# Second feed-forward layer on one core: order of the sums of factors, of the copies of finished blocks, and of the last scaling

## The chip, the cores and the metric

The kernel runs on one core of a Trainium2 chip. The core has five engines with queues of their own: TensorE (PE: matmuls, and PEld for loading their weights), VectorE (DVE), ScalarE (ACT), GpSimd (POOL) and SyncE (SP), which here issues most transfers. Sixteen DMA engines move data between the main memory and the core's SBUF; matmuls write to PSUM, which has eight banks of 128 x 512 float32 numbers. The metric is the device time of one execution in microseconds (us), given as the median of several runs.

## The reference

The program is one layer of a diffusion trunk: a mixer with a gated linear recurrence, then a feed-forward part with a convolution, each with a normalisation ahead and a gated residual behind, and a last normalisation. Only the end matters here:

```python
def conv_ffn(h, w_up, conv_w, conv_b, w_down):
    u = dwconv(h @ w_up, conv_w, conv_b)
    gate, val = jnp.split(u, 2, axis=-1)
    return (jax.nn.silu(gate) * val) @ w_down

def rmsnorm(x, g):
    xf = x.astype(jnp.float32)
    y = xf * lax.rsqrt(jnp.mean(xf * xf, axis=-1, keepdims=True) + EPS)
    return (y * g).astype(x.dtype)
...
    lat = lat + g2 * conv_ffn(hl, ffn_w_up[l], ffn_conv_w[l], ffn_conv_b[l], ffn_w_down[l])
...
return rmsnorm(lat, final_g)
```

The second feed-forward layer is the product with `w_down`: 2048 tokens x 2816 by 2816 x 1024. The result is multiplied by the gate g2, added to the residual stream, normalised over its 1024 columns and scaled by `final_g`.

## The kernel before

**A product in seven.** The matrix of hidden values (2048 x 2816) and `w_down` (2816 x 1024) are each cut in two by two blocks. Instead of eight block products the kernel makes seven, from sums and differences of blocks (a scheme of the Strassen kind). Tokens are dealt to the two row blocks by tiles of 128: even tiles to one, odd tiles to the other. A block product is 1024 x 1408 by 1408 x 512.

**Steps and phases.** The inner dimension of 1408 is cut into `NC` = 11 slices of 128. One slice of one block product is a *step*. The first six products are phases 0 to 5, so steps 0 to 65 (`for s in range(N)`, L1721, `ph, c = divmod(s, NC)`). In a step a *left factor* (128 x 1024: the transposed hidden values of eight token tiles) meets a *right factor* (128 x 512). There are eight output blocks `ys[j]` of 128 x 512, one in each PSUM bank. The seventh product runs last, in another order: block after block, each in a piece of eight slices and one of three (`pieces`, L1755), so that each block of tokens can be finished and stored while the next is computed.

**High and low parts.** A float32 factor is split in a high part (rounded, by ACT, L78) and a low part (what the rounding left, by DVE, L79). `product` (L1634) makes three matmuls of it: high by high (L1637), high by low (L1638), low by high (L1639). The tiles are called `mh` and `ml` for the left factor, three buffers each, and `wd` for the right one, both parts in one tile. While the first two matmuls of a step run, the low part of its left factor may still be missing; the third one needs it.

**Sums.** In phases 1 to 3 the left factor is the sum or difference of two blocks (L1598, tiles `S` and `lr`; `lr` has four buffers, and phase 3 needs two a step). In phases 1, 2, 3 and 5 the right factor is a difference (L1627, tiles `rr` and `u2`, two buffers each); in phases 1 and 2 the difference is also stored by SP (L1629), for a later phase. All these sums are made by DVE, in place.

**Run-ahead.** `ahead(s)` (L1710) is traced once a step, before the products of the step. It traces the loads of left factors up to step s+3 and of right ones up to step s+5, then the left factors up to s+2 (`make_left`, L1595) and the right ones up to s+4 (`make_right`, L1624). The order in which each engine issues is not the order of the text: a planner goes through the program with its own estimates of durations and issues, on each engine, what is ready first, with the earlier text first among what is ready. So a sum, whose inputs come from memory, can be queued well ahead of a low part that stands earlier in the text, and once queued it holds its engine until its inputs are there: the engines issue in the planned order.

**End of a phase.** `phase_end` (L1666) empties the eight blocks: in phases 0 to 3 ACT copies them (to `P`, `X`, `V` and tiles `lr`), in phases 4 and 5 DVE adds them to `P` and `X`. Phases 1, 2 and 3 go on in the banks of the phase before, adding to what is there, so that they can write block j only when block j has been copied; phases 0, 4 and 5 start afresh, in banks that must have been emptied. What is to be done afterwards with each block (a subtraction, gate and residual, squares) is put into the list `later` and traced one item a step.

**The end.** `finish` (L1656) sums the two squares, makes the scale with one multiplication and addition on DVE and one power on POOL (`rms_scale`, L72), then scales both halves of a token tile on DVE (L1663, times scale, times `final_g`) and stores each by SP (L1664). Even tiles are finished after their last piece (L1774 to L1778), odd ones through `later`.

Of the kernel before, what the change touches and what calls it, by code (L numbers as in the profile page):

```python
# [11 lines left out]
F32 = mybir.dt.float32  # L12
# [3 lines left out]
AF = mybir.ActivationFunctionType  # L16
OP = mybir.AluOpType
# [4 lines left out]
D = 1024  # L22
# [7 lines left out]
EPS = 1e-6  # L30
# [15 lines left out]
def body(ctx, tc, a, out):  # L46
    nc = tc.nc
    pe, act, dve, pool, sp = nc.tensor, nc.scalar, nc.vector, nc.gpsimd, nc.sync
# [20 lines left out]
    mhalf = small("mhalf")  # L69
# [7 lines left out]
    def split(h, l, src):  # L77
        i = act.activation(h, src, AF.Copy)  # L78
        j = dve.tensor_tensor(l, src, h.bitcast(F32), OP.subtract)  # L79
        return i.ins, j.ins  # L80
# [955 lines left out]
    NC = NFF // 2  # L1036
# [312 lines left out]
    wk = pool_(fa, "wka", 2)  # L1349
# [152 lines left out]
    for g, (half, s, n, q, pairs) in enumerate(todo):  # L1502
# [3 lines left out]
        w, r = pairs[q].w.pop(LEFT[n]), rhs[n]  # L1506
        if n == "B11":
            z = bank["a", q] = ps.tile([128, HJ, 128], F32, name="za", tag="za")
# [3 lines left out]
        elif n == "T2":  # L1512
            z = ps.tile([128, HJ, 128], F32, name="zb", tag="zb")
            acc_mm(z, w, r, True)
            dve.tensor_tensor(u2s[q], u2s[q], z, OP.add)
        elif n == "T1":
            z = bank["d", q] = ps.tile([128, HJ, 128], F32, name="zd", tag="zd")
# [3 lines left out]
        elif n == "T3":  # L1521
            z = bank["c", q] = ps.tile([128, HJ, 128], F32, name="zc", tag="zc")
            acc_mm(z, w, r, True)
            dve.tensor_tensor(cols(uvs[q], 1), cols(uvs[q], 1), z, OP.add)  # L1524
        elif n == "B21":
            z = bank["a", q]
# [26 lines left out]
    def gate_rows():  # L1553
# [32 lines left out]
    def left_split(s, width, src, **kw):  # L1586
        h = mk.tile([128, HALF], F32R, name="mh", tag="mh", bufs=3)
        l = mk.tile([128, HALF], F32R, name="ml", tag="ml", bufs=3)
        lefts[s] = h, l
        h, l = h[:, 0:width], l[:, 0:width]  # L1590
        if kw:
            h, l = [v.rearrange("p (c n) -> p c n", **kw) for v in (h, l)]
        split(h, l, src)

    def make_left(s, raw):  # L1595
        ph = s // NC
        if 1 <= ph <= 3:
            dve.tensor_tensor(raw[0], raw[0], raw[1], OP.add if ph == 1 else OP.subtract)  # L1598
# [25 lines left out]
    def make_right(s, raw):  # L1624
        ph, c = divmod(s, NC)
        if len(raw) > 1:
            dve.tensor_tensor(raw[0], raw[0], raw[1], OP.subtract)  # L1627
            if ph < 3:
                sp.dma_start(t_d[ph - 1][c], raw[0])  # L1629
        if ph > 4:  # L1630
            gate2(ph - 5, raw[0])
        right_split(s, raw[0])

    def product(z, l, r, start, stop):  # L1634

        (lh, ll), (rh, rl) = l, r
        pe.matmul(z, lh, rh, start=start, stop=False, skip_group_check=True)  # L1637
        pe.matmul(z, lh, rl, start=False, stop=False, skip_group_check=True)  # L1638
        pe.matmul(z, ll, rh, start=False, stop=stop, skip_group_check=True)  # L1639
# [4 lines left out]
    def residual2(t, dh, v):  # L1644

        cs = slice(dh * 512, (dh + 1) * 512)
        lat = wk.tile([128, 512], F32, name="latd", tag="latd", bufs=3)
        sp.dma_start(lat, lat_d[t][:, cs])
        gate2(dh, v)
        dve.tensor_tensor(v, v, lat, OP.add)  # L1650

    def square(t, dh, v):
        sq = wk.tile([128, 512], F32, name="sq", tag="sq", bufs=1)
        act.activation(sq, v, AF.Square, accum_out=sums[:, dh, t:t + 1])

    def finish(t, vs):  # L1656
        ss = wk.tile([128, 1], F32, name="ssf", tag="ssf", bufs=2)
        rs = wk.tile([128, 1], F32, name="rsf", tag="rsf", bufs=2)
        dve.tensor_tensor(ss, sums[:, 0, t:t + 1], sums[:, 1, t:t + 1], OP.add)
        rms_scale(rs, ss, 1, D)  # L1660
        for i, v in enumerate(vs):
            cs = slice(i * 512, (i + 1) * 512)
            dve.scalar_tensor_tensor(v, v, rs, st["fg"][:, cs], OP.mult, OP.mult)  # L1663
            sp.dma_start(out[t * 128:(t + 1) * 128, cs], v)  # L1664

    def phase_end(ph, ys):  # L1666

        for j, z in enumerate(ys):
            if ph == 0:
                act.activation(P[:, j], z, AF.Copy)  # L1670
            elif ph == 1:
                act.activation(X[:, j], z, AF.Copy)  # L1672
                later.append(lambda j=j: dve.tensor_tensor(X[:, j], P[:, j], X[:, j], OP.subtract))
            elif ph == 2:
                act.activation(V[:, j], z, AF.Copy)
                later.append(lambda j=j: residual2(2 * j, 1, V[:, j]))
            elif ph == 3:
                if j % 2 == 0:
                    st["w", j] = st["w", j + 1] = left_raw()
                w = st["w", j][:, j % 2 * 512:(j % 2 + 1) * 512]  # L1680
                act.activation(w, z, AF.Copy)
                st["c22", j] = w

                def c22(j=j, w=w):
                    dve.tensor_tensor(X[:, j], X[:, j], w, OP.add)
                    residual2(2 * j + 1, 0, X[:, j])
                    residual2(2 * j + 1, 1, w)
                    square(2 * j + 1, 1, w)
                later.append(c22)
            elif ph == 4:  # L1690
                dve.tensor_tensor(P[:, j], P[:, j], z, OP.add)  # L1691

                def c11(j=j):
                    residual2(2 * j, 0, P[:, j])
                    square(2 * j, 0, P[:, j])
                later.append(c11)
            else:
                dve.tensor_tensor(X[:, j], X[:, j], z, OP.add)

                def c21(j=j):  # L1700
                    square(2 * j + 1, 0, X[:, j])
                    finish(2 * j + 1, (X[:, j], st["c22", j]))
                later.append(c21)

    later = []
    raws_l = {s: None for s in range(2)}
# [3 lines left out]
    def ahead(s):  # L1710
        for t in range(len(raws_l), min(s + 4, N if s >= 4 else 6)):
            raws_l[t] = load_left(t)
        for t in range(len(raws_r), min(s + 6, N + NC)):
            raws_r[t] = load_right(t)
        for t in range(len(lefts), min(s + 3, N)):
            make_left(t, raws_l[t])
        for t in range(len(rights), min(s + 5, N + NC)):
            make_right(t, raws_r[t])

    S = V = None  # L1720
    for s in range(N):  # L1721
        ph, c = divmod(s, NC)
        if s == 4:
            for f in pending:
                f()
            fa.close()
            wk = pool_(fb, "wkb")
            S = wk.tile([128, NC, HT, 128], F32, name="S")
        if s == 4 * NC // 2:
            V = h2p.tile(ST, F32, name="V", tag="rB21", bufs=1)  # L1730
        if s == NC // 2 + 1:
            st["g2"], st["fg"], gate_bias = gate_rows()
        if s == 2 * NC - 2:
# [30 lines left out]
    for i, (j, cs) in enumerate(pieces):  # L1764
        prepare_last(i + 2)
        if cs.start == 0:
            z = ps.tile([128, 512], F32, name="y", tag="y")
        l = lefts[N + i]
        for n, c in enumerate(cs):
            js = slice(n * 128, (n + 1) * 128)  # L1770
            product(z, [v[:, js] for v in l], rights[N + c], c == 0, c == NC - 1)
        if later and i % 2 == 0:
            later.pop(0)()
        if cs.start:  # L1774
            v = V[:, j]
            dve.tensor_tensor(v, v, z, OP.add)  # L1776
# [30 lines left out]
```

## Time and profile before

| | us |
|---|---|
| median of 3 runs | 2758.75 |
| the runs | 2753.68 to 2759.02 |
| the profiled execution | 2759.34 |
| its span in the profile | 2757.3 |
| first matmul of this stage starts | 2322.7 |
| last matmul starts | 2749.84 |
| TensorE busy, whole span | 2708.4 (98%) |
| DVE busy, whole span | 1976.0 (72%) |
| ACT busy, whole span | 1129.5 (41%) |

The stage thus takes 427 us of the 2757. Rows of the profile name the engine, the line of the kernel, the operation and what it writes and reads (`ml<-S,mh` writes ml from S and mh). In the view in order of time the first number is the start, the second the duration, and a bracket at the end says how long the engine stood idle before and what released it. In the view of groups, `xN | busy, mean ns | idle before` follow the shape. In the view of waits, the numbers are us in total, how often, and the longest. The view of windows gives the busy time of each engine in a stretch. The granted clock of TensorE is full throughout. Matmuls overlap: each is shown at 0.39 us, but a new one starts every 0.227 us.

### The profile page before, as it was taken

Reading aid. Unit: us, or ns where it says so; the run is one execution under the profiler, and the core shown is the slowest. Engines: PE = TensorE matmul, PEld = TensorE weight load, DVE = VectorE, ACT = ScalarE, POOL = GpSimd, SP = SyncE. Lnnn points to the kernel's source line nnn. Section 1 sums busy time; section 2 is a strip of 40 time slices with the busy share of each in tenths; the row PEclk is TensorE's granted clock in tenths of the full one; section 3 lists DMA queues with packets and bytes.
Section 4 is the critical chain, followed back from the end, with each engine's and each line's share of the span. In section 5 each row is a group of like instructions: output and inputs, shape, how many; then the busy total and the mean of one; then the engine's idle time right before and its main releaser. Section 6 shows DMA issues by size and latency. Waiting matters only on the chain. (4 is left out here: it accounts for less than half of the span.)

```text
span 2757.3 us, 42014 instructions
## 1 busy us (share of the span) xinstructions
PE 2708.4 (98%) x16060; PEld 2254.6 (82%) x16060; DVE 1976.0 (72%) x2791; ACT 1129.5 (41%) x1885; POOL 568.2 (21%) x885
## 2 busy tenths in 40 slices
PE   6999999999999999999999999999999999999998
PEld 4888888888888888888887888888888888877887
DVE  4756655566666776668886887777877777586886
ACT  4424443333233233335665444444444444333343
POOL 2111111011111111211220533443434440000001
PEclk9999999999999999999999999999999999999999
DMA  5213323224534443228888222228322234987563
GB/s 230 92 51 100 104 85 100 85 71 168 172 123 136 149 137 112 86 84 295 298 305 323 92 92 68 86 77 305 93 72 81 77 92 151 319 294 249 186 194 122
DMA packets 229104, 410.56 MB, mean 149 GB/s; under 512 B 29604, under 2 KB 137508, under 8 KB 225064
## 3 DMA queue, kind: packets, MB, share of 16 engines
q1 hardware_dynamic: 224584, 398.13, 43.6%
q10 hardware_dynamic: 4320, 9.77, 0.9%
q8 instruction: 126, 2.06, 0.3%
q14 instruction: 74, 0.61, 0.1%
HBM read 293.23 MB, written 114.57 MB: 148 GB/s over the span
## 5 line engine op out<-in xcount | busy, mean ns | idle before, releaser
L445 PE MATMUL z<-tok,w 128*128 128x512 f32 x1280 | 515.4, 403 | 0.0
L447 PE MATMUL z<-tok,w 128*128 128x512 f32 x1280 | 501.0, 391 | 0.0
L446 PE MATMUL z<-tok,w 128*128 128x512 f32 x1280 | 500.8, 391 | 0.0
L79 DVE TENSOR_TENSOR w<-raw,w 128x512 fp32r<-128x512 f32 (+1 forms) x260 | 239.6, 925 | 138.0 <-ACT w L78 134.0
L447 PEld LDWEIGHTS z<-tok,w 128*128 128x128 f32 x1280 | 240.4, 188 | 51.8
L445 PEld LDWEIGHTS z<-tok,w 128*128 128x128 f32 x1280 | 240.7, 188 | 46.0 <-issue 1.7
L446 PEld LDWEIGHTS z<-tok,w 128*128 128x128 f32 x1280 | 241.1, 188 | 45.0 <-DVE tok L79 0.9
L78 ACT ACTIVATE w<-raw 128x512 fp32r<-128x512 f32 (+1 forms) x260 | 196.0, 759 | 138.9 <-PE zd L1061 77.4
L1639 PE MATMUL y<-wd,ml 128*128 128x512 f32 x600 | 234.4, 391 | 2.8 <-DVE ml L79 2.7
L1637 PE MATMUL y<-wd,mh 128*128 128x512 f32 x600 | 233.8, 390 | 2.6 <-ACT X L1672 1.8
L1638 PE MATMUL y<-wd,mh 128*128 128x512 f32 x600 | 233.5, 389 | 0.0
L514 DVE TENSOR_TENSOR_SCAN S<-F,d 128x528 f32<-128x528 f32 (+1 forms) x80 | 91.5, 1143 | 113.3 <-ACT F L496 113.2
L79 DVE TENSOR_TENSOR w<-s,w 128x512 fp32r<-128x512 f32 x126 | 121.3, 968 | 52.8 <-ACT w L78 52.0
L1058 PE MATMUL zc<-rT,w 128*128 128x512 f32 x352 | 137.1, 389 | 1.2 <-DVE uv L1524 1.0
L1060 PE MATMUL zc<-rT,w 128*128 128x512 f32 x352 | 136.9, 389 | 0.0
L1061 PE MATMUL zc<-rT,w 128*128 128x512 f32 x352 | 136.9, 389 | 0.0
L1639 PEld LDWEIGHTS y<-wd,ml 128*128 128x128 f32 x600 | 112.6, 188 | 29.3 <-DVE ml L79 5.9
L1637 PEld LDWEIGHTS y<-wd,mh 128*128 128x128 f32 x600 | 112.6, 188 | 27.0 <-ACT X L1672 2.2
L78 ACT ACTIVATE w<-s 128x512 fp32r<-128x512 f32 x126 | 78.2, 627 | 137.6 <-POOL s L1114 81.0
L75 POOL TENSOR_TENSOR rs<-rs,mhalf 128x1 f32<-128x1 f32 (+3 forms) x53 | 61.7, 1165 | 345.0 <-DVE rs L74 345.0
L1638 PEld LDWEIGHTS y<-wd,mh 128*128 128x128 f32 x600 | 112.6, 188 | 23.2
L1058 PE MATMUL za<-rB,w 128*128 128x512 f32 x336 | 130.7, 389 | 0.0
(353 smaller groups left out, 6246.8 us busy)
## 6 DMA issues: line engine op xcount, KB each, us to landing
raw<-in_w_up_dram SPq DMA_DIRECT2D x88, 512.0 KB, 4.1
raw<-in_w_in_dram SPq DMA_DIRECT2D x80, 512.0 KB, 4.0
lr<-m SPq DMA_DIRECT2D x49, 512.0 KB, 6.0
m<-r SPq DMA_DIRECT2D x66, 256.0 KB, 4.1
spare<-in_w_ada_dram SPq DMA_DIRECT2D x32, 512.0 KB, 4.3
kq<-stash SPq DMA_DIRECT2D x15, 1024.0 KB, 7.8
og<-stash SPq DMA_DIRECT2D x30, 512.0 KB, 5.3
u<-in_w_down_dram SPq DMA_DIRECT2D x51, 256.0 KB, 4.2
```

Source lines behind the costliest of these rows:

```text
L78: i = act.activation(h, src, AF.Copy)
L79: j = dve.tensor_tensor(l, src, h.bitcast(F32), OP.subtract)
L445: pe.matmul(z, w[:, 0, k], h, start=k == 0, stop=False, skip_group_check=True)
L446: pe.matmul(z, w[:, 0, k], l, start=False, stop=False, skip_group_check=True)
L447: pe.matmul(z, w[:, 1, k], h, start=False, stop=k == KT - 1, skip_group_check=True)
L514: dve.tensor_tensor_scan(flat(S[:, d]), flat(F[:, d]), flat(d1[:, 0:ns]), 0.0, OP.mult, OP.max)
L1058: pe.matmul(o, w[:, 0, k], r[:, :, 0, k], start=start and k == 0, stop=False, skip_group_check=True)
L1060: pe.matmul(o, w[:, 0, k], r[:, :, 1, k], start=False, stop=False, skip_group_check=True)
L1061: pe.matmul(o, w[:, 1, k], r[:, :, 0, k], start=False, stop=k == 3, skip_group_check=True)
L1637: pe.matmul(z, lh, rh, start=start, stop=False, skip_group_check=True)
L1638: pe.matmul(z, lh, rl, start=False, stop=False, skip_group_check=True)
L1639: pe.matmul(z, ll, rh, start=False, stop=stop, skip_group_check=True)
```

## The change

Three things are changed, all in the second feed-forward layer.

1. *Sums tied behind the last low part.* `left_split` now keeps the instruction that makes the low part. A left or right sum, and in phases 0 to 3 the item of `later` too, is traced inside `behind_left()`: its DVE instructions may not be issued ahead of the low part that was traced last. `tc.issue_after(i)` adds an order within i's engine, no wait for its end. With the order of the text, the left sum of step s+3 comes behind the low part of step s+2, and the right sum of step s+4 behind the low part of step s+2.
2. *Finished blocks one by one.* `phase_end` takes one block and is traced directly behind that block's last product, in place of all eight behind the step. Its instruction for block 7 is kept, and all that the next `ahead` traces on the same engine (ACT after phases 0 to 3, DVE after phase 4) is tied behind it. No item of `later` is traced in the last step of a phase.
3. *Last scaling.* `last_finish` takes the place of addition, square and `finish` for the even tiles. P's half is multiplied by `final_g` ahead of the scale; the first square's part of the scale is made ahead; V's half is multiplied by `final_g` into a tile of its own after the addition; the scale is then one DVE operation and the power; DVE scales V's half and SP stores it, ACT scales P's half and stores it from its own queue.

```diff
+    made_left, ended = [], []
+
+    def behind_left():
+        return tc.issue_after(made_left[-1]) if made_left else ExitStack()
...
-        split(h, l, src)
+        made_left.append(split(h, l, src)[1])
 
     def make_left(s, raw):
         ph = s // NC
         if 1 <= ph <= 3:
-            dve.tensor_tensor(raw[0], raw[0], raw[1], OP.add if ph == 1 else OP.subtract)
+            with behind_left():
+                dve.tensor_tensor(raw[0], raw[0], raw[1], OP.add if ph == 1 else OP.subtract)
...
         if len(raw) > 1:
-            dve.tensor_tensor(raw[0], raw[0], raw[1], OP.subtract)
+            with behind_left():
+                dve.tensor_tensor(raw[0], raw[0], raw[1], OP.subtract)
...
-    def phase_end(ph, ys):
-
-        for j, z in enumerate(ys):
-            if ph == 0:
-                act.activation(P[:, j], z, AF.Copy)
...
+    def phase_end(ph, j, z):
+
+        if ph == 0:
+            i = act.activation(P[:, j], z, AF.Copy)
...
+        return i.ins
...
         if s >= 2:
-            ahead(s)
+            with ExitStack() as tied:
+                for i in ended:
+                    tied.enter_context(tc.issue_after(i))
+                ended.clear()
+                ahead(s)
...
             product(ys[j], [v[:, js] for v in l], r, c == 0 and ph in (0, 4, 5), c == NC - 1)
+            if c == NC - 1:
+                ended[:] = [phase_end(ph, j, ys[j])]
...
-        if later:
-            later.pop(0)()
-        if c == NC - 1:
-            phase_end(ph, ys)
+        if later and c < NC - 1:
+            with behind_left() if ph < 4 else ExitStack():
+                later.pop(0)()
...
+    def last_finish(t, v, p, z):
+        vg = wk.tile([128, 512], F32, name="latd", tag="latd", bufs=3)
+        ss = wk.tile([128, 1], F32, name="ssf", tag="ssf", bufs=2)
+        rs = wk.tile([128, 1], F32, name="rsf", tag="rsf", bufs=2)
+        dve.tensor_scalar(ss, sums[:, 0, t:t + 1], 1.0 / D, EPS, OP.mult, OP.add)
+        dve.tensor_tensor(p, p, st["fg"][:, 0:512], OP.mult)
+        dve.tensor_tensor(v, v, z, OP.add)
+        square(t, 1, v)
+        dve.tensor_tensor(vg, v, st["fg"][:, 512:], OP.mult)
+        dve.tensor_scalar(rs, sums[:, 1, t:t + 1], 1.0 / D, ss, OP.mult, OP.add)
+        pool.tensor_tensor(rs, rs, mhalf[:, 0:1], OP.pow)
+        dve.tensor_scalar(vg, vg, rs, None, OP.mult)
+        sp.dma_start(out[t * 128:(t + 1) * 128, 512:], vg)
+        act.activation(p, p, AF.Copy, scale=rs)
+        act.dma_start(out[t * 128:(t + 1) * 128, 0:512], p)
...
-            v = V[:, j]
-            dve.tensor_tensor(v, v, z, OP.add)
-            square(2 * j, 1, v)
-            finish(2 * j, (P[:, j], v))
+            last_finish(2 * j, V[:, j], P[:, j], z)
```

More of the change, by code (lines that the diff above doesn't have):

```diff
@@ L1664, in finish @@
             sp.dma_start(out[t * 128:(t + 1) * 128, cs], v)
-    def phase_end(ph, ys):
-        for j, z in enumerate(ys):
-            if ph == 0:
-                act.activation(P[:, j], z, AF.Copy)
[L1671 to L1703, printed above, removed]
@@ new lines, in phase_end, with c22, c11, c21 @@
+    def phase_end(ph, j, z):
+        if ph == 0:
+            i = act.activation(P[:, j], z, AF.Copy)
+        elif ph == 1:
+            i = act.activation(X[:, j], z, AF.Copy)
+            later.append(lambda j=j: dve.tensor_tensor(X[:, j], P[:, j], X[:, j], OP.subtract))
+        elif ph == 2:
+            i = act.activation(V[:, j], z, AF.Copy)
+            later.append(lambda j=j: residual2(2 * j, 1, V[:, j]))
+        elif ph == 3:
+            if j % 2 == 0:
+                st["w", j] = st["w", j + 1] = left_raw()
+            w = st["w", j][:, j % 2 * 512:(j % 2 + 1) * 512]
+            i = act.activation(w, z, AF.Copy)
+            st["c22", j] = w
+            def c22(j=j, w=w):
+                dve.tensor_tensor(X[:, j], X[:, j], w, OP.add)
+                residual2(2 * j + 1, 0, X[:, j])
+                residual2(2 * j + 1, 1, w)
+                square(2 * j + 1, 1, w)
+            later.append(c22)
+        elif ph == 4:
+            i = dve.tensor_tensor(P[:, j], P[:, j], z, OP.add)
+            def c11(j=j):
+                residual2(2 * j, 0, P[:, j])
+                square(2 * j, 0, P[:, j])
+            later.append(c11)
+        else:
+            i = dve.tensor_tensor(X[:, j], X[:, j], z, OP.add)
+            def c21(j=j):
+                square(2 * j + 1, 0, X[:, j])
+                finish(2 * j + 1, (X[:, j], st["c22", j]))
+            later.append(c21)
+        return i.ins
```

## The prediction

> **What bounds it now.** I read the page first, then the waits of TensorE in the second feed-forward layer, then the engines' order of time around each wait, and last the end.
>
> ```profile
> span 2757.3 us, 42014 instructions
> PE 2708.4 (98%) x16060; PEld 2254.6 (82%) x16060; DVE 1976.0 (72%) x2791; ACT 1129.5 (41%) x1885; POOL 568.2 (21%) x885
> ...
> L1637 PE MATMUL y<-wd,mh x600: 387/389/504, 2333.6 to 2749.4; 128*128 128x512 f32 x150
> ...
> L1637 PE MATMUL y<-wd,ms x16: 389/389/389, 2322.7 to 2332.9; 128*128 128x512 f32 x16
> ...
> 2449.88 0.39 PE L1637 MATMUL y<-wd,mh 128*128 128x512 f32 x1
> ...
> 2455.32 0.39 PE L1637 MATMUL y<-wd,mh 128*128 128x512 f32 x1
> ...
> 2749.84 0.39 PE L1639 MATMUL y<-wd,ml 128*128 128x512 f32 x1
> ```
>
> TensorE is the bound: only what shortens its row, or what follows its last matmul, moves the end. The stage has 616 products of three matmuls (600 + 16 rows of the first), 1848 in all. Undisturbed, 24 of them (one step) take 2455.32 - 2449.88 = 5.44 us, 0.2267 each. From 2322.7 to 2749.84 are 427.1 us; 1847 distances of 0.2267 are 418.7. So **8.4 us** are lost in this stage: the most that the reordering can win. The page's 98% hides it. Whom TensorE waited for there (first column after the colon: us in total):
>
> ```profile
> PE y L1639 <- DVE ml L79: 2.7, 4, 0.7
> PE y L1637 <- ACT X L1672: 1.8, 1, 1.8
> PE y L1637 <- DVE P L1691: 0.9, 2, 0.7
> ```
>
> These idle times count less than the loss, because the matmul that restarts is slower and short waits are not listed. I take each place from matmul starts instead.
>
> **Part 1: finished blocks copied one by one, new factors behind them.** End of phase 1:
>
> ```profile
> 2441.14 0.58 ACT L1672 ACTIVATE X<-y 128x512 f32<-128x512 f32 x1
> 2443.07 0.69 DVE L1627 TENSOR_TENSOR rr<-rr,u 128x512 f32<-128x512 f32 x1
> 2443.80 0.63 ACT L78 ACTIVATE wd<-rr 128x512 fp32r<-128x512 f32 x1 [2.09 <-DVE rr L1627]
> 2444.34 3.02 ACT L1672 ACTIVATE X<-y 128x512 f32<-128x512 f32 x6
> ...
> 2442.81 0.39 PE L1639 MATMUL y<-wd,ml 128*128 128x512 f32 x1
> 2444.97 0.50 PE L1637 MATMUL y<-wd,mh 128*128 128x512 f32 x1 [1.77 <-ACT X L1672]
> 2445.30 0.39 PE L1638 MATMUL y<-wd,mh 128*128 128x512 f32 x1
> ```
>
> ACT's queue holds a right factor (wd) between the copies of block 0 and block 1. The factor waits for its sum on DVE, the sum for loads; the copies stand behind, and the next phase may not write block 1 until it is copied. Lost: (2444.97 - 2442.81 - 0.227) + (2445.30 - 2444.97 - 0.227) = **2.04 us**. With the change this sum is queued behind a low part that is itself made from a high part queued behind the copy of block 7, so the factor cannot slip in. A copy lasts 0.58 and starts every 0.5 us in the row of six; TensorE finishes a block every 0.68. The copies therefore keep up, and I count all 2.04. What is late next: the high part tied to block 7 starts about 0.7 us into the step and is needed two steps (10.9 us) later; high part 1.04 and low part 1.22 fit.
>
> End of phase 4, where DVE empties the blocks:
>
> ```profile
> 2628.45 0.68 DVE L1691 TENSOR_TENSOR P<-P,y 128x512 f32<-128x512 f32 x1
> 2629.04 1.22 DVE L79 TENSOR_TENSOR ml<-ug,mh 128x1024 fp32r<-128x1024 f32 x1
> ...
> 2628.71 0.39 PE L1639 MATMUL y<-wd,ml 128*128 128x512 f32 x1
> 2629.27 0.47 PE L1637 MATMUL y<-wd,mh 128*128 128x512 f32 x1 [0.18 <-DVE P L1691]
> ...
> 2629.81 0.40 PE L1639 MATMUL y<-wd,ml 128*128 128x512 f32 x1
> 2630.91 0.50 PE L1637 MATMUL y<-wd,mh 128*128 128x512 f32 x1 [0.70 <-DVE P L1691]
> ```
>
> Distances of 0.56 and 1.10 instead of 0.227: **1.2 us** (the slower restarts stand in the rest, below). A low part of 1.22 splits the additions of blocks 0 and 1, which come late already. That low part is traced ahead of them and not tied; but its high part no longer waits on ACT behind a right factor made ahead of its turn, so it comes sooner. I count 1.2; the lower bound is 0, if the same low part still splits the additions.
>
> **Part 2: sums behind the last low part.** The rest of the 8.4, **5.2 us**, are waits for low parts. The clearest is step 40:
>
> ```profile
> 2540.10 1.05 ACT L78 ACTIVATE mh<-lr 128x1024 fp32r<-128x1024 f32 x1
> ...
> 2545.20 1.22 DVE L1598 TENSOR_TENSOR lr<-lr 128x1024 f32<-128x1024 f32 x1 [4.28 <-DMA lr<-m]
> 2546.34 1.22 DVE L79 TENSOR_TENSOR ml<-lr,mh 128x1024 fp32r<-128x1024 f32 x1
> ...
> 2547.62 0.50 PE L1639 MATMUL y<-wd,ml 128*128 128x512 f32 x1 [0.67 <-DVE ml L79]
> ```
>
> The high part is done at 2541.2, and DVE could make the low part at once. It stands for 4.28 us on the sum of the next step instead, whose load has not landed. Tied, that sum comes behind, the low part ends near 2542.4 and its buffer is reloaded 5 us sooner. The tie adds no instruction, only order. What moves with it: in phases 1 and 2 each right sum issues a store on SP, now later; SP's queue is in order, so reloads behind that store wait too (rival c). The postponed work is tied as well. In phase 3's first seven steps DVE carries a left sum 1.22, a low part 1.22, a right sum and a right low part (0.69 each, as in the row at 2443.07) and, with two more operations of that size, gate and residual: 5.2 of 5.44 us. That is nearly full; but a delay falls on the work queued behind the low part, which no matmul of the next two steps reads.
>
> The price is lead. A sum for a right factor now goes no earlier than the low part two steps before it, hence at most about four steps minus 3 us ahead of use, some 19 us. Before, they ran farther: the sum of step 14 starts at 2369.6 (row under the rivals), for a step that begins near 2398.8 (2449.88, where step 23 begins, less nine steps and the 2.04 lost), 29 us. Loads spread out accordingly, and phase 3's first seven steps must carry two left loads, two right ones and a latent block: 3.5 times 512 KB, 1.835 MB in 5.44 us, or 337 GB/s.
>
> ```profile
> lr<-m SPq DMA_DIRECT2D x49, 512.0 KB, 6.0
> ...
> 2398.90:2409.70 10.80, 10.80 (x49) 8.95 (x48) 6.16 (x8) 3.16 (x4) 0.00 (x0) 1.00 0.90 314
> 2409.70:2420.60 10.90, 10.90 (x50) 9.01 (x48) 7.92 (x10) 3.17 (x4) 0.00 (x0) 1.00 0.97 339
> ...
> 2714.40:2725.30 10.90, 10.90 (x50) 9.03 (x49) 8.56 (x19) 3.71 (x8) 2.14 (x4) 1.00 0.28 105
> ```
>
> (Windows: last columns clock, DMA share, GB/s.) The engines gave 339 GB/s at a share of 0.97 and 314 at 0.90, so that demand stands at the top of what these windows show. At 314, a step takes 5.84 us, 0.4 late, 2.8 us over seven steps; at 339, nothing. Low parts will be up to 8.6 us ahead on entry (two steps minus 2.3), which should swallow either. I leave **1.0 us** of the 5.2 in place, between 0 (all covered) and 2.8 (none), nearer the first because of that lead. Won: 4.2.
>
> The Trainium skill, "DMA: Bandwidth & Descriptors", section "Where 436 GB/s comes from", puts the port ceiling at 435 GB/s and the share of HBM near 358. By either there is headroom over 337 and the 1.0 us would be zero, the sum then 1.0 larger; the windows here top out at 339 with the engines 97% busy, so I keep the row's bound.
>
> **Part 3: last scaling on two engines.** Before, after the last matmul:
>
> ```profile
> 2751.05 0.63 ACT L1654 ACTIVATE sq<-V 128x512 f32<-128x512 f32 x1 [6.00 <-DVE V L1776]
> ...
> 2752.00 0.15 DVE L74 TENSOR_SCALAR rsf<-ssf 128x1 f32<-128x1 f32 x1
> 2752.30 0.55 POOL L75 TENSOR_TENSOR rsf<-rsf,mhalf 128x1 f32<-128x1 f32 x1 [4.53 <-DVE rsf L74]
> 2752.88 0.75 DVE L1663 SCALAR_TENSOR_TENSOR P<-P,rsf,gt 128x512 f32<-128x512 f32 x1 [0.73 <-POOL rsf L75]
> ...
> 2754.32 0.33 SPq L1664 DMA_DIRECT2D out_dram<-V  x1
> ...
> L1199 DVE TENSOR_SCALAR xn<-lat,rs 128x1024 f32<-128x1024 f32 x16 | 11.9, 746 | 1.4 <-POOL rs L75 1.0 <-POOL ug L1369 0.4
> L107 ACT ACTIVATE xt<-xt,rs 128x1024 f32<-128x1024 f32 x8 | 9.2, 1150 | 15.1 <-POOL rs L75 15.1
> ```
>
> One small operation instead of two stands between the square and the power: 0.15 and its hand-over, 0.2, less. The power then ends at 2752.65. The products with the final gain are off the path: P's is made before the last block ends, V's (0.69, two inputs of that size) beside the square of 0.63 and its read-out. The two scalings run side by side: DVE, half of the 0.75 row plus overhead, about 0.45; ACT, like the 0.63 square of the same size (bounds 0.58 for half the 1.15 row, 1.15 for all of it). ACT's store is issued near 2753.4, the last of the two; SP's was at 2754.32. Won: **0.95**, between 0.4 (ACT at 1.15) and 1.15. For the seven tiles before the last, DVE gets about 0.3 us more and ACT 0.6 per 7.5 us; the last window above has them at 8.56 and 3.71 of 10.9, so this costs nothing, and at most those 0.3 a tile (2 us) if DVE had no room.
>
> **The sum.** 2.04 + 1.2 + 4.2 + 0.95 = 8.4 us. The profiled execution took 2759.34 (span 2757.3 and 2.0 around it), which is 0.6 above the median of 2758.75: it becomes 2750.9, the median **2750.3**.
>
> **Rivals.** (a) The waits for low parts stay under another name: the sum no longer blocks DVE, but in phase 3 low parts still wait for late left loads (for: lr took 6.0 us at the median, 512 KB; against: the high part of step 40 was ready 5 us early). Then 3.2 + 0.95 = 4.2 are won: 2754.6. (b) The end of part 1 and the tail fail and only part 2 acts, 4.2: 2754.6; I give it little, for both chains are in plain view. (c) Slower: the lead of right factors runs out. Two buffers hold them, and each reload waits for the split and, in phases 1 and 2, for the store of the sum.
>
> ```profile
> L1627 DVE TENSOR_TENSOR rr<-rr,u x12: 684/691/693, 2369.6 to 2429.7; 128x512 f32<-128x512 f32 x12
> ```
>
> Twelve sums over 60.1 us are 5.46 each, a hair over the step's 5.44, while free to run. If the tie lengthens that loop, the spare 17 us (19 minus 2 for the split) are gone after 22 sums at 17 / 22 = 0.77 more, a pace of 6.2. From there each further 0.1 costs 2.2 us; at 6.9 the loss is 15, less the 8.4 won: 2765.5. Against it: the loop has two steps, 10.9 us, for a sum of 0.69, a split of 0.63 and 0.69 and the transfers, and the tie adds to none of these. (d) Nothing measurable: runs before span 2753.68 to 2759.02, so 0.2% (5.5 us) is about the smallest change to be told from none.
>
> **How the numbers follow.** Forecast 0.62; (a) and (b) 0.20; (c) 0.12; (d) 0.06. Faster by over 0.2% holds most of the forecast and a little of (a): 0.64; within: 0.23; slower: 0.13. The range: the forecast alone spans 2748 to 2752.5 by the bounds of parts 1 to 3, and down to 2745 if the lower of the runs before is the usual one (2753.68 - 8.4); upward it takes (a), (b) and (d), to 2760. Case (c) is left out.
>
> **What would show it.** Right: no wait of L1637 for X or P copies, of L1639 for low parts at most 1 us; 427.1 falls below 421; DVE's sums idle for loads while low parts are already made; the last stores go out about 2.3 us after the power's start. Wrong: a wait of TensorE for wd (case c), matmul waits in phase 3 with left loads at 7 us or more (a), or copies still interrupted by a factor.

## The result, and the profile after

| us | before | after |
|---|---|---|
| median (nine runs each, side by side) | 2758.75 | 2751.21 |
| lowest and highest | 2753.68 to 2760.39 | 2749.08 to 2753.99 |
| profiled execution | 2759.34 | 2749.08 |
| span in the profile | 2757.3 | 2747.2 |
| first to last matmul start of the stage | 427.16 | 419.68 |
| last matmul start to the end of the span | 7.46 | 6.95 |

The ratio of the runs is 0.998, with a 95% interval of 0.9971 to 0.9989: between 3.0 and 8.0 us faster, with the middle at 5.5. The medians differ by 7.5, near the upper end. The forecast was 2750.3, 0.9 below what came.

The page of the changed kernel, the rows of its matmuls with first and last start, and all that TensorE waited for in the stage:

```profile
span 2747.2 us, 41999 instructions
PE 2704.9 (98%) x16060; PEld 2253.5 (82%) x16060; DVE 1976.5 (72%) x2799; ACT 1138.4 (41%) x1893; POOL 567.1 (21%) x885
...
L1644 PE MATMUL y<-wd,ms x16: 389/389/389, 2320.6 to 2330.8; 128*128 128x512 f32 x16
...
L1646 PE MATMUL y<-wd,ml x600: 387/389/397, 2331.9 to 2740.3; 128*128 128x512 f32 x150
...
PE y L1645 <- DVE wd L79: 0.2, 1, 0.2
```

Of the three kinds of wait that were there before (low parts, X copies, P additions) none is left; one of 0.2 us for a right factor is new. From 2320.57 to 2740.25 are 419.7 us. In what follows, **lost** means the time from the stage's first to its last matmul start, less the 418.7 of an undisturbed stage: 8.5 before (the prediction's 8.4 is the same, from 427.1), 1.0 after.

The two spans differ by 10.1 us: 7.5 in the stage, 0.5 in the tail, and 2.1 ahead of the stage, which begins at 2320.6 instead of 2322.7. Nothing was changed there. Those 2.1 us are a difference between two executions, and the profile after is the lowest of its nine runs while the one before stands 0.6 above its median. That is why the spans differ by more than the medians.

### The profile page after: what moved, and what is told of

It is laid out like the page before. It is cut to its first block, busy times and chain, and to the rows that moved or that the text cites. A ratio compares the mean times of both kernels' runs of the same rounds, so it can differ in the third digit from the quotient of the medians.

```text
span 2747.2 us, 41999 instructions
## 1 busy us (share of the span) xinstructions
PE 2704.9 (98%) x16060; PEld 2253.5 (82%) x16060; DVE 1976.5 (72%) x2799; ACT 1138.4 (41%) x1893; POOL 567.1 (21%) x885
## 4 chain that ended last, share of the span: by engine, by line
PE 80%; DVE 2%; DMA 1%; ACT 1%; issue 1%; POOL 0%; ACTq 0%; SPq 0%; POOLq 0%; DVEq 0%
PE z L445 8%; PE z L447 8%; PE z L446 8%; PE y L1646 5%; PE y L1645 5%; PE y L1644 5%; PE zd L1058 3%; PE zd L1061 3%; PE zd L1060 3%; PE zc L1058 3%; PE zc L1061 3%; PE zc L1060 3%; PE za L1061 3%; PE za L1058 3%; PE za L1060 3%; PE y L1183 2%
```

## The experiments

Three sets of kernels ran, each set beside its own runs of the kernel before (median 2757.07 of 31, 2755.3 of 31, and 2755.0 of 25 runs). Half the width of an interval is some 2.5 us, so the medians tell only the large differences; "lost" and "tail" (last matmul start to the end) come from one profiled execution each, whose own time stands beside them.

| kernel | median | ratio (95%) | profiled | lost | tail |
|---|---|---|---|---|---|
| e1_sums_only | 2751.07 | 0.9981 (0.9972 to 0.999) | 2751.09 | 1.1 | 7.84 |
| e2_ends_only | 2753.02 | 0.9985 (0.9976 to 0.9994) | 2754.07 | 4.4 | 7.46 |
| e3_tail_only | 2754.0 | 0.9992 (0.9982 to 1.0001) | 2754.1 | 5.7 | 6.95 |
| e4_no_end_tie | 2751.33 | 0.998 (0.9971 to 0.999) | 2752.58 | 3.3 | 6.95 |
| e5_right_untied | 2749.26 | 0.9977 (0.9968 to 0.9986) | 2747.75 | 0.0 | 6.95 |
| e6_left_untied | 2755.38 | 1.0003 (0.9993 to 1.0012) | 2754.62 | 6.5 | 6.95 |
| e7_lead2 | 2753.1 | 0.9992 (0.9982 to 1.0001) | 2754.64 | 4.4 | 7.40 |
| e8_lead1 | 2759.11 | 1.0013 (1.0003 to 1.0023) | 2758.07 | 9.7 | 6.99 |
| e9_left_only | 2751.95 | 0.9988 (0.9978 to 0.9997) | 2748.47 | 0.0 | 7.84 |
| e10_right_free_one_queue | 2748.85 | 0.998 (0.9971 to 0.999) | 2748.7 | 0.7 | 7.02 |
| e11_right_free_one_engine | 2749.01 | 0.9978 (0.9969 to 0.9987) | 2748.52 | 0.0 | 7.08 |
| e12_before_again | (one run) | | 2754.86 | 5.1 | 7.46 |

**Each part alone.** The kernel before with the ties of part 2 only:

```diff
...
-        split(h, l, src)
+        made_left.append(split(h, l, src)[1])
...
-            dve.tensor_tensor(raw[0], raw[0], raw[1], OP.add if ph == 1 else OP.subtract)
+            with behind_left():
+                dve.tensor_tensor(raw[0], raw[0], raw[1], OP.add if ph == 1 else OP.subtract)
...
-            dve.tensor_tensor(raw[0], raw[0], raw[1], OP.subtract)
+            with behind_left():
+                dve.tensor_tensor(raw[0], raw[0], raw[1], OP.subtract)
...
-            later.pop(0)()
+            with behind_left() if ph < 4 else ExitStack():
+                later.pop(0)()
```

> The kernel before with part 2 alone (left sums, right sums and the postponed items tied behind the last low part). 'Lost' is the time from the first to the last matmul start of the stage, less 418.7 us; before 8.4, changed kernel 1.0. Theory (order on DVE caused the waits for low parts): lost about 3.2 to 3.5, that is the 2.0 at the end of phase 1 and 1.2 to 1.4 at the end of phase 4 stay, no wait for ml; tail from last matmul start to the end of the span stays 7.5; time about 5 us under before. Rival (late loads cause them): ml waits stay, lost 7 or more, gain under 1.5 us. Second rival (the ties of sums also cure the ends of the phases, because the factor between the copies can no longer be hoisted): lost 1 to 2.

The changed kernel without these ties and with the old tail, so that part 1 alone is left:

```diff
-            with behind_left():
-                dve.tensor_tensor(raw[0], raw[0], raw[1], OP.add if ph == 1 else OP.subtract)
+            dve.tensor_tensor(raw[0], raw[0], raw[1], OP.add if ph == 1 else OP.subtract)
...
-            with behind_left():
-                dve.tensor_tensor(raw[0], raw[0], raw[1], OP.subtract)
+            dve.tensor_tensor(raw[0], raw[0], raw[1], OP.subtract)
...
-            last_finish(2 * j, V[:, j], P[:, j], z)
+            v = V[:, j]
+            dve.tensor_tensor(v, v, z, OP.add)
+            square(2 * j, 1, v)
+            finish(2 * j, (P[:, j], v))
```

> The kernel before with part 1 alone (blocks emptied one by one, the next step's factors tied behind block 7). Theory (the two parts are separate): lost about 5.2, the waits for ml stay, those for X and P go; gain about 3.2 us. Rival (part 1 only works when the sums are tied, since factors of later steps are free to be queued between the copies): lost 8 or so, the waits for X or P stay, gain within 1 us.

The kernel before with part 3 only:

```diff
-            v = V[:, j]
-            dve.tensor_tensor(v, v, z, OP.add)
-            square(2 * j, 1, v)
-            finish(2 * j, (P[:, j], v))
+            last_finish(2 * j, V[:, j], P[:, j], z)
```

> The kernel before with part 3 alone (last scaling on two engines). Theory by the trace of the changed kernel: lost stays 8.4, tail from last matmul start to the end of the span 6.9 to 7.0 instead of 7.5, gain about 0.5 us, not to be told from none in the times. By the prediction's step: tail 6.5, gain 0.95. Rival (the added work on DVE and ACT delays the last loop): waits of TensorE in the last loop, lost over 9.

And the changed kernel in which the work behind a phase's end is not tied to the copy of block 7:

```diff
-                for i in ended:
-                    tied.enter_context(tc.issue_after(i))
```

> The changed kernel without the tie of the next step's factors behind block 7; blocks still traced one by one, sums still tied. Theory (the tie keeps the factor out of the copies): the wait for X at the end of phase 1 returns in part, lost 2 to 3. Rival (the tied sums alone keep the factors back, the tie behind block 7 is not needed): lost about 1.0 as in the changed kernel, time equal to it.

TensorE's waits in the stage, with part 1 alone, then without the tie of the ends:

```profile
PE y L1644 <- DVE ml L79: 2.5, 4, 0.8
...
```

```profile
PE y L1644 <- ACT X L1678: 1.2, 2, 0.9
PE y L1645 <- DVE wd L79: 0.4, 1, 0.4
...
```

With part 1 alone the X and P waits are gone and the low parts' stay; without the tie to block 7 the X waits come back while the low parts' stay away. But the parts do not add. The sums alone lose 1.1 us: of their waits only one of 0.2 us for a right factor is listed, so they also remove most of what was put down to part 1. The ends alone lose 4.4. The medians repeat it: 6.0, 4.1 and 3.1 us won by sums, ends and tail come to 13, where all three together won 7.5 (beside other runs of the kernel before). The tail's 3.1 cannot be told from noise: its trace wins 0.5, and its interval includes no gain.

**Which tie.** The left or the right sum was taken out of the changed kernel's ties:

```diff
-            with behind_left():
-                dve.tensor_tensor(raw[0], raw[0], raw[1], OP.subtract)
+            dve.tensor_tensor(raw[0], raw[0], raw[1], OP.subtract)
```

> The changed kernel with the right sums free again, left sums and postponed items still tied. Lost = first to last matmul start of the stage less 418.7 us; changed kernel 1.0, before 8.5 in its one profile and 5.7 in the tail-only kernel, whose order up to the last loop is that of before. Theory (both kinds of sums stood ahead of low parts: in before, of the eight low parts that were late, three came behind a right sum): lost 2.5 to 4, waits for ml in phase 2 behind L1634. Rival (the left sums alone did it): lost about 1.0.

```diff
-            with behind_left():
-                dve.tensor_tensor(raw[0], raw[0], raw[1], OP.add if ph == 1 else OP.subtract)
+            dve.tensor_tensor(raw[0], raw[0], raw[1], OP.add if ph == 1 else OP.subtract)
```

> The changed kernel with the left sums free again, right sums and postponed items still tied. Theory: lost 2.5 to 4, waits for ml in phase 3 behind L1604 that waits for lr. Rival (the right sums alone did it, because the left sums follow the loads and these follow the right sums): lost about 1.0.

Without the left tie the whole gain is gone (1.0003), although ends, right tie and tail are all in. The trace shows how, at the end of phase 1: the wait, then DVE, ACT and TensorE in order of time, then a window of 4 us (the third column from the end is the granted clock):

```profile
PE y L1643 <- ACT X L1677: 3.7, 1, 3.7
...
2439.10 1.23 DVE L1603 TENSOR_TENSOR S<-S,lr 128x1024 f32<-128x1024 f32 x1 [2.75 <-DMA lr<-m]
2440.25 1.22 DVE L79 TENSOR_TENSOR ml<-S,mh 128x1024 fp32r<-128x1024 f32 x1
2441.38 0.68 DVE L1633 TENSOR_TENSOR rr<-rr,u 128x512 f32<-128x512 f32 x1
...
2442.10 0.63 ACT L78 ACTIVATE wd<-rr 128x512 fp32r<-128x512 f32 x1 [6.46 <-DVE rr L1633]
2443.58 2.53 ACT L1677 ACTIVATE X<-y 128x512 f32<-128x512 f32 x5
...
2440.16 0.39 PE L1645 MATMUL y<-wd,ml 128*128 128x512 f32 x1
2444.21 0.71 PE L1643 MATMUL y<-wd,mh 128*128 128x512 f32 x1 [3.66 <-ACT X L1677]
2444.71 0.63 PE L1644 MATMUL y<-wd,mh 128*128 128x512 f32 x1
2445.14 0.63 PE L1645 MATMUL y<-wd,ml 128*128 128x512 f32 x1
...
2444.00:2448.00 4.00, 3.79 (x10) 3.00 (x11) 4.00 (x5) 2.27 (x6) 0.00 (x0) 0.57 0.95 291
```

A left sum holds DVE for 2.75 us until its load has landed. The low part stands behind it, the tied right sum behind the low part, the factor on ACT (6.46 us idle) behind that sum, the copies of X behind the factor, and TensorE behind the copies: a wait that began as a left sum's appears as a wait for X. By this order the right tie should make it worse, for it joins the right factors to a queue that left sums can block; that is argued, and fits with the ends alone (neither tie), which had no such wait and lost 4.4. The waits for low parts that were expected here did not come. Whether the right tie keeps them away, or the standstill, in which loads could catch up, is not shown.

Without the right tie nothing is lost at all: in that trace TensorE waits for nothing in the stage. (The next kernel with free right sums, below, does have one wait of 0.5 us for X, so the zero is one execution's.)

The right tie has a price that the waits hardly show. In the seventh product the six kernels with it lose, by one trace each, 0.7 us (changed kernel), 0.6 (sums only), 1.4 (no end tie), 1.0 (left untied), 4.5 and 6.9 (the two with less lead, below); the eight without it lose nothing there. The changed kernel and e5_right_untied differ in this tie alone.

So the tie of the left sum was tried by itself, in the kernel before:

```diff
...
-        split(h, l, src)
+        made_left.append(split(h, l, src)[1])
...
-            dve.tensor_tensor(raw[0], raw[0], raw[1], OP.add if ph == 1 else OP.subtract)
+            with behind_left():
+                dve.tensor_tensor(raw[0], raw[0], raw[1], OP.add if ph == 1 else OP.subtract)
```

> The kernel before with one thing added: the left sums tied behind the last low part. Theory after the runs so far (the left tie is the cause of nearly all that is won in the stage): lost 0 to 2, no wait for ml, time 4 to 6 us under before, tail 7.5. Rival (the end-of-phase parts are needed beside it): lost 3 or more, with waits for X or P.

Its first and last matmul rows:

```profile
L1643 PE MATMUL y<-wd,ms x16: 389/389/389, 2320.2 to 2330.4; 128*128 128x512 f32 x16
...
L1645 PE MATMUL y<-wd,ml x600: 388/389/393, 2331.6 to 2738.9; 128*128 128x512 f32 x150
```

2738.9 - 2320.2 = 418.7: one tie of one sum can remove every stall of the stage, the ends included. That this execution is the lowest of ten, 3.5 us under its median, forbids to claim more: at the medians the one tie wins 3.1 us (0.8 to 6.1 by the interval), the kernels that have the new ends and tail as well 6.0 to 6.2. That the rest of the change wins something in other executions is likely and not shown.

**The lead of the right factors.** Rival (c) was made to happen, by letting right factors be made only up to step s+2, and s+1, in place of s+4:

```diff
-        for t in range(len(rights), min(s + 5, N + NC)):
+        for t in range(len(rights), min(s + 3, N + NC)):
```

> The changed kernel with right factors made up to s+2 in place of s+4 (loads as before): two steps less lead for the sums that are tied. Theory (the lead of 19 us, 17 spare, is far more than is needed: in the changed kernel each right sum runs right behind its low part, paced by TensorE and not by the loads): lost about 1.0 to 1.5, time that of the changed kernel. Rival c of the prediction (the lead is what covers the loop of sum, store and reload): two steps less take 10.9 us of the 17, and any pace over 5.7 us a step shows as waits for wd, lost over 3.

```diff
-        for t in range(len(rights), min(s + 5, N + NC)):
+        for t in range(len(rights), min(s + 2, N + NC)):
```

> The changed kernel with right factors made up to s+1 only. Theory: the right factor of step s+1 is made in step s behind the low part of s+2, at 2.3 us plus sum 0.69, high 0.63, low 0.69, so it ends 4.4 us into a step of 5.44 and about 1 us is spare: some waits for wd, lost 2 to 6. By rival c the loop itself is too slow: waits for wd in nearly every step of phases 1 and 2, lost over 10, slower than before.

TensorE's waits at lead 2, then those at lead 1 with two of the longest in order of time:

```profile
PE y L1644 <- ACT wd L78: 1.9, 2, 1.4
```

```profile
PE y L1644 <- ACT wd L78: 3.3, 4, 1.5
PE y L1644 <- ACT mh L78: 1.0, 1, 1.0
...
2627.85 1.43 PE L1644 MATMUL y<-wd,mh 128*128 128x512 f32 x5 [1.49 <-ACT wd L78]
2694.39 0.73 PE L1644 MATMUL y<-wd,mh 128*128 128x512 f32 x2 [1.00 <-ACT wd L78]
```

With a lead of one step phases 1 to 3, where the rival had its loop of two buffers with store and reload, lose 0.5 us. The loss is at the start of step 56 (1.8) and above all from 2685 to 2713 (some 7), in the last product: there a new right factor is needed every 0.7 us until all eleven are made, not every 5.4. Lead 2 loses all its 4.4 between 2684 and 2702. So the mechanism is real, but at another place. It makes the kernel slower than before (1.0013) only with three of the four steps of lead gone, yet with the full lead some 0.7 us are already lost at that place.

**The tail.** On the kernel with free right sums, first both stores by SP, then both scalings by DVE as well:

```diff
-        act.dma_start(out[t * 128:(t + 1) * 128, 0:512], p)
+        sp.dma_start(out[t * 128:(t + 1) * 128, 0:512], p)
```

> The changed kernel with free right sums (as in the fifth run) and both last stores issued by SP, scalings still on DVE and ACT. Theory (a store issued from ACT lands 0.43 us later than one from SP, 2.46 against 2.03 from issue): the second store is issued at about 3.7 us after the last matmul's start, lands at 5.7 instead of 6.0, tail 6.65 instead of 6.95. Rival (the last store lands later because two fly at once): tail unchanged, 6.9 or more. In the times not to be told from the fifth run.

```diff
-        act.activation(p, p, AF.Copy, scale=rs)
-        act.dma_start(out[t * 128:(t + 1) * 128, 0:512], p)
+        dve.tensor_scalar(p, p, rs, None, OP.mult)
+        sp.dma_start(out[t * 128:(t + 1) * 128, 0:512], p)
```

> The same with both last scalings on DVE, V's half first, and both stores by SP. By rows of the changed kernel (0.49 a scaling, 0.44 apart, 0.33 an issue): second store issued 3.75 us after the last matmul's start, tail 6.7. If two engines are worth what the prediction took them for, the tail is 7.0 or more.

Neither is told from the other, or from two engines, by its time. The issues of the last stores, with the second one's time to landing from the view of transfers, first of the changed kernel, then with one queue, then the first store of the kernel before:

```profile
2740.25 0.39 PE L1646 MATMUL y<-wd,ml 128*128 128x512 f32 x1
2743.03 0.72 ACT L1780 ACTIVATE P<-P,rsf 128x512 f32<-128x512 f32 x1 [0.91 <-POOL rsf L1777]
2743.03 0.49 DVE L1778 TENSOR_SCALAR latd<-latd,rsf 128x512 f32<-128x512 f32 x1 [0.66 <-POOL rsf L1777]
2743.55 0.33 SPq L1779 DMA_DIRECT2D out_dram<-latd  x1
2743.78 0.34 ACTq L1781 DMA_DIRECT2D out_dram<-P  x1
...
out_dram<-P ACTq DMA_DIRECT2D x1, 256.0 KB, 2.5
```

```profile
2743.14 0.33 SPq L1778 DMA_DIRECT2D out_dram<-latd  x1
2743.57 0.38 SPq L1780 DMA_DIRECT2D out_dram<-P  x1
...
out_dram<-P SPq DMA_DIRECT2D x1, 256.0 KB, 2.3
```

```profile
2753.66 0.33 SPq L1664 DMA_DIRECT2D out_dram<-P  x1
...
out_dram<-V SPq DMA_DIRECT2D x3, 256.0 KB, 2.0
```

| | before | after | one queue | one engine |
|---|---|---|---|---|
| first store after the last matmul start | 3.82 | 3.30 | 3.35 | 3.42 |
| second store behind the first | 0.66 | 0.23 | 0.43 | 0.43 |
| second store to its landing | 2.03 | 2.46 | 2.27 | 2.28 |
| first store to the second's landing | 2.69 | 2.69 | 2.70 | 2.70 |

The last row is the same in all four: the sooner the second store goes out, the longer it takes. The first store of the last two is 0.05 and 0.12 later for a reason ahead of the scalings, which start 2.84 and 2.91 us after the last matmul start, in place of 2.78. The DMA engines in the 3 us from 2743.4 in the changed kernel, in slices of 0.075 us:

```profile
DMA  0000000000000899999997999999999410000000
GB/s 0 0 0 0 0 0 0 0 0 0 0 0 0 273 355 410 410 437 410 382 382 300 410 355 382 437 382 382 382 355 382 137 28 0 0 0 0 0 0 0
```

They are busy without a gap for 1.35 us, from about 0.8 us after the first issue to the end of the second transfer: two times 256 KB at some 390 GB/s. A second store issued up to 0.66 us after the first waits for the engines, from whatever queue it comes. The longer tails of the big table (7.84 twice, where 7.5 was expected, and 7.40) lie behind the landing: there the span ends 1.33 to 1.41 us after it, in the others 0.95 to 1.00. Why is not shown.

**The kernel before once more**, unchanged:

> The kernel before once more, for a second profile of it. If its loss in the stage were set by the order alone, lost is 8.5 again; the tail-only kernel, with the same order up to the last loop, lost 5.7, so the theory is that it depends on when the loads land: 5 to 9, with waits at other steps.

TensorE's waits in the stage:

```profile
PE y L1639 <- DVE ml L79: 1.7, 2, 0.9
PE y L1637 <- ACT X L1672: 1.3, 1, 1.3
```

With the same instructions in the same order it lost 5.1 us in place of 8.5, and the tail-only kernel, whose order is that of the kernel before up to its last product, 5.7. By place, from the matmul starts:

| us lost | before | before again | tail only |
|---|---|---|---|
| end of phase 1 (X copies) | 2.0 | 1.6 | 1.3 |
| end of phase 4 (P additions) | 1.4 | 0.2 | 0.0 |
| the rest (low parts) | 5.0 | 3.3 | 4.4 |

The waits for X and for low parts stay, with other sizes; the loss at the end of phase 4 was all but gone without any change. Chains like that of step 40 begin at a load, so it is likely, and not shown, that the sizes go by when the loads land.

## Why the prediction was right, and where it was not

**What bounds it: right.** "The most that the reordering can win" was 8.4 us, from 427.1 against 418.7. Three kernels of the study ran the stage at 418.7, so that floor is real. What the prediction did not see is that 8.4 was one execution's: 5.1 and 5.7 in the two others seen. From these the change would win 4.6 and 5.2 (less the 1.0 that is left, plus 0.5 in the tail), from the profile before 8.0. The medians gave 7.5, and in the later sets 5.7 to 6.2 for the kernels nearest to the change. So it is partly luck that the forecast came within 0.9 us: the loss was taken from the execution that lost most, the runs before had a higher median (2758.75) in this set than in the three later ones (2755.0 to 2757.07), and the terms below err in both directions. The gain of 4.2 us by rivals (a) and (b) lies inside the interval of 3.0 to 8.0, too; only the traces decide against them.

Two signs from the prediction's list for "wrong" did appear, each at a price of at most 0.7 us: a factor between the copies, and a wait of TensorE for a right factor.

**Part 1, end of phase 1: the loss goes, for another reason than given.** "The factor cannot slip in" is wrong. ACT's rows and TensorE's after the change:

```profile
2438.88 1.55 ACT L1678 ACTIVATE X<-y 128x512 f32<-128x512 f32 x3
2441.31 0.63 ACT L78 ACTIVATE wd<-rr 128x512 fp32r<-128x512 f32 x1 [0.88 <-DVE rr L1634]
2441.85 2.53 ACT L1678 ACTIVATE X<-y 128x512 f32<-128x512 f32 x5
...
2442.07 0.39 PE L1646 MATMUL y<-wd,ml 128*128 128x512 f32 x1
2442.48 0.50 PE L1644 MATMUL y<-wd,mh 128*128 128x512 f32 x1
```

A factor still stands between the copies of block 2 and block 3. It is traced a step earlier than the copies, so the tie to block 7 does not hold it. But three copies are already through, ACT idles only 0.88 us for its sum, and the cost is 0.29 us in place of 2.04. Won: 1.75.

**Part 1, end of phase 4: the reason was right, the size one execution's.** DVE's additions and low parts, and TensorE's first matmul of phase 5:

```profile
2615.55 0.69 DVE L1697 TENSOR_TENSOR P<-P,y 128x512 f32<-128x512 f32 x1 [1.19 <-PE y L1646]
2616.15 1.22 DVE L79 TENSOR_TENSOR ml<-ug,mh 128x1024 fp32r<-128x1024 f32 x1
...
2617.89 0.68 DVE L1697 TENSOR_TENSOR P<-P,y 128x512 f32<-128x512 f32 x1
...
2620.89 2.48 DVE L1697 TENSOR_TENSOR P<-P,y 128x512 f32<-128x512 f32 x4
2623.28 1.22 DVE L79 TENSOR_TENSOR ml<-ug,mh 128x1024 fp32r<-128x1024 f32 x1
...
2620.11 0.39 PE L1644 MATMUL y<-wd,mh 128*128 128x512 f32 x1
```

A low part still splits the additions of blocks 0 and 1. But it is made 4.0 us before phase 5 begins, in place of 0.1 after (2629.04 against 2628.94, one distance behind the last matmul of phase 4 at 2628.71), and the addition of block 0 starts 4.6 us before, in place of 0.5. So it holds up nothing, and between 2619.7 and 2627.8 every matmul starts 0.227 us after the one before. The 1.2 us are gone in this trace, but two executions with the old order lost only 0.2 and 0.0 there.

**Part 2: right in sum, wrong on which tie and on what is left.** No wait for a low part is left: all of the 5.2 us went, not 4.2. The 1.0 "left in place" for phase 3 is not there. Windows of two steps in phase 3, and DVE's order in one of them:

```profile
2517.00:2528.00 11.00, 11.00 (x50) 9.13 (x49) 9.66 (x13) 3.51 (x5) 0.00 (x0) 1.00 0.96 334
2528.00:2539.00 11.00, 11.00 (x51) 9.09 (x50) 9.66 (x14) 4.03 (x6) 0.00 (x0) 1.00 0.97 335
...
2528.74 1.23 DVE L79 TENSOR_TENSOR ml<-lr,mh 128x1024 fp32r<-128x1024 f32 x1 [0.68 <-ACT mh L78]
2529.89 0.69 DVE L1634 TENSOR_TENSOR rr<-rr,u 128x512 f32<-128x512 f32 x1
...
2531.09 1.22 DVE L1604 TENSOR_TENSOR lr<-lr 128x1024 f32<-128x1024 f32 x1
```

The demand was sized well: 334 and 335 GB/s at shares of 0.96 and 0.97, where 337 was worked out. DVE is nearly as full as foreseen (9.66 of 11.00, where 5.2 of 5.44 a step was worked out). No matmul of phase 3 starts more than 0.227 us after the one before: the bound "0" holds. The engines delivered what was asked in the time of a step, so nothing here shows that the lead of the low parts was needed. The order is the one the tie asks for, low part, right sum, left sum; but DVE idles for high parts of ACT (0.68), not for loads, as the list of signs had it.

The prediction treated left and right sums alike. The left tie carries the gain (6.5 lost without it). The right one carries none that a run shows: its benefit was taken for granted, and its price, put at nothing in the sum, is the 0.6 to 1.4 us at the last product. Of the 1.0 us lost after the change, 0.29 is at the end of phase 1 and the rest in the last product, most of it at the one listed wait:

```profile
2686.84 0.69 DVE L79 TENSOR_TENSOR wd<-u,wd 128x512 fp32r<-128x512 f32 x1
...
2687.58 0.50 PE L1645 MATMUL y<-wd,mh 128*128 128x512 f32 x1 [0.22 <-DVE wd L79]
```

Rival (c) looked for such a wait in phases 1 to 3; no step of the prediction looked here. The experiments on the lead show it to be the stage's next tight place.

**Part 3: mechanism right, one term mis-sized.** 0.95 was forecast, 0.51 came. The issue of the last store stands just where the sum had it: 3.53 us after the last matmul start (2743.78 - 2740.25) in place of 4.48, 0.95 sooner. The term that failed is its landing, taken to be that of the store before: 2.46 instead of 2.03, because it now waits for the other half's transfer. What counts is when the first store goes out, and that came 0.52 sooner. So neither the second engine nor the second queue earns anything measurable. Of the 0.52, half (0.26) is won ahead of the scalings, mostly by one small operation less; the other half between the start of the first scaling and the first issue (0.52 us in place of 0.78), because the product with the final gain is made beforehand. The sign "about 2.3 us after the power's start" contradicted the prediction's own sum, which makes it 1.3; the trace has 1.33 (2743.78 - 2742.45).

**The rivals.** (a) fell: no wait for a low part is left, and the left loads took 5.2 us at the median:

```profile
lr<-m SPq DMA_DIRECT2D x49, 512.0 KB, 5.2
```

(b) named 4.2 us for part 2 alone; the sums alone lost 1.1 us in the stage, so that part is worth more by itself. (c) exists, at the last product: with the lead that the change leaves it costs 0.7 us there, far from the 15 that the rival named. (d), no change, is outside the interval, though the interval reaches below the 5.5 us that (d) took for the smallest change to be told from none.

## What to carry to other kernels

An engine that issues in a fixed order pays for an instruction whose input is late with everything queued behind it; look for ready work behind a waiting one, and order that single pair before adding ties elsewhere: here one tie was enough to remove every wait in one trace, and a second one cost 0.6 to 1.4 us and won nothing that a run shows. The name in the list of waits is the end of such a chain: X copies here waited, three steps back, for a left sum's load. Before splitting a last store over engines or queues, see whether the DMA engines are already busy without a gap from the first byte to the last.

## What the runs showed of the hardware

- Of two 256 KB stores issued 0.23 to 0.66 us apart the second lands 2.69 to 2.70 us after the first issue, by one queue or by two, in all fourteen traces; the two move at some 390 GB/s; the long windows of loads in phase 3 top out at 335.
- After the 3.66 us of idleness shown above, matmuls started 0.427 us apart (2444.71 to 2445.14) until 2447.70, 3.5 us after the restart, and 0.23 apart from then on; the granted clock of that window is 0.57. That adds some 1.7 us to the wait: eight distances took 3.49 us in place of 1.81. After the wait of 1.77 us at the end of phase 1 before, only the first distance was longer (0.33). The Trainium skill, "TensorE: Matmul & The Clock Gate", section "Part 1: The HAM clock gate (the "warmup" mystery)", has the array at half clock until some 3.4 us of work have passed; this trace agrees, with 3.5 us.
- One order of instructions lost 5.1, 5.7 and 8.5 us in three executions. A loss read from one profile is a sample, and here it was the largest of the three.
